# A hybrid S5 and stick-breaking attention block on Trainium2: the tiles on the left side of SBUF lie 32 bytes further on

## The chip, the cores and the metric

The kernel runs on one core of a Trainium2 chip (trn2). The metric is the device time of one execution in microseconds, and the kernel before takes 1482.84 us as the median of three runs (1481.27 to 1486.74). The engines are named as in the profile: PE is TensorE's matmuls and PEld its weight loads, DVE is VectorE, ACT is ScalarE, POOL is GpSimd, and SP issues most of the DMAs.

SBUF is the on-chip memory: 128 partitions, in each of which a tile has a start address in bytes. A matmul reads two operands from SBUF. The stationary one (128 columns here) is put into the array by a weight load; the streamed one then runs through it, up to 512 columns at a time. The result goes to PSUM.

## The reference

One layer, a sequence of 2048 tokens of width 1024, all in float32. From the reference, cut:

```python
hn = rmsnorm(h, mix_norm_g[i])
proj = hn @ w_in[i]
u, g_ssm, q, k, v, g_attn = jnp.split(proj, SPLITS, axis=-1)
y_ssm = s5_branch(u, ...) * jax.nn.silu(g_ssm)
y_att = stick_breaking_branch(q, k, v, q_norm_g[i], k_norm_g[i]) * jax.nn.silu(g_attn)
h = h + jnp.concatenate([y_ssm, y_att], axis=-1) @ w_out[i]
ple_gate = jax.nn.sigmoid(rmsnorm(h, ple_norm_g[i]) @ w_ple_gate[i])
h = h + ple_gate * (p[i] @ w_ple_proj[i])
```

The S5 branch is a diagonal complex state-space model in 32 groups, followed by a GELU and a gated linear unit. The attention has 8 heads of 64, and its weights are products of sigmoids over the keys between a key and the query.

## The kernel before, in words

**The products.** Matmuls that need more precision than one pass gives are done in three: both operands are split into a high and a low part (`split`, line 511; type float32r), and `mm3` and `mm3x` (lines 536 and 702) add high x high, high x low and low x high. So a group of matmuls stands on three lines of the profile: 541 to 543 for `mm3`, 707 to 709 for `mm3x`. Other matmuls are plain float32, and PE also does the transposes (lines 526, 340, 999).

**The stages, in order of time.**

- `phase_u` (line 546) loads x and the first weights and makes u (ps_u). The weights w_w are stationary, and the tokens xt, 256 columns at a time, are streamed.
- Eight batches of the state-space model (`ssm_pack`, `ssm_batch`), with `gate_unit` (line 642) between them: ps_sg, with w_w stationary and xt or xg streamed. Two blocks of attention projections (ps_qk, line 733) lie here too.
- Attention over four passes of two heads. `attn_proj` (line 712) makes q, k, v and the gate from tokens xt (stationary) and weights w_w (streamed, 512 columns): ps_q, line 745. It uses the array in two halves of 64 rows side by side, so its matmuls come in pairs. `attn_block` (line 795) makes the scores ps_z (line 812: q stationary, k streamed, in groups of three pairs), scans them on DVE (line 821), transposes them (ps_wt) and multiplies by v (ps_o, line 843).
- The gated linear unit, `glu_unit` (line 684), among the last attention blocks: ps_g and ps_v, with w_w stationary and zr streamed.
- `phase_out` (line 1037): `mixed_pair` makes ps_h from W_out and `gated_pair` ps_g from the gate's weights, both through `cross_products` (line 903), which needs seven half-size products instead of eight. Its stationary operand is yr, which is made from the tokens; the streamed one is a weight tile: w_w (products 0 to 3), wx (4) or w_wc (5 and 6). ps_p multiplies p by its weights: pr stationary, w_wp streamed.

**Where tiles lie.** Tiles come from pools. A pool opened without a side grows from the left end of SBUF upwards, one opened with `side="right"` from the right end downwards, and a pool that is closed leaves its room to the next. In order, the pools on the left are const, then w (the weights w_w, 16 tiles of 4096 bytes), stage, then gx with pu, stage1 or pb, later xp with kv2, wx and glu, at the end fin with fstage. On the right are kv0, proj, keep, chain or pack, later kv1 and attn, at the end w3, hr and gstage. The tiles that the matmuls read lie so:

| tile | pool | side | made or loaded at |
|---|---|---|---|
| w_w | w, wx | left | line 478 |
| xt, xg | gx, xp | left | 553, 589, 646, 716 |
| zr | glu | left | 674 |
| yr | fin | left | 916 |
| wx | xp | left | 888 |
| k | kv0 (slot 0), kv1 (1, 3, 4) | right | 769 |
| k | kv2 (slots 2, 5, 6, 7) | left | 769 |
| q | proj | right | 770 |
| w_wc, w_wp | w3 | right | 478 |
| pr | hr | right | 1005 |

The first pool, const, holds ten small tiles of a few bytes to 512 bytes a partition. Each takes a slot of whole multiples of 32 bytes. Everything on the left begins where const ends, so what const holds sets all the addresses on that side; pools on the right count from the other end (line 1331: `first, last = 16512, 229344`).

**The order of the work.** Each engine has its own queue. The order within each is not that of the code: the program's instructions are planned by a list scheduler (`plan`, `list_schedule`, `best_order`, `arrange`, lines 1328 to 1568), which takes costs from `duration` and dependencies from overlaps of tiles, and fixes the order on each engine.

The tile that the change touches is `warm` (lines 1081 to 1083). It is set to zero, and one sigmoid on it puts ACT's table in place at the start. Nothing reads it later.

Of the kernel before, what the change touches and what calls it, by code (L numbers as in the profile page):

```python
# [18 lines left out]
P = 128  # L19
# [1030 lines left out]
def hybrid_block_kernel(ctx: ExitStack, tc: tile.TileContext, x, xt, small, p, w_in, ssm_w_glu, w_out, w_ple_gate,  # L1050
# [27 lines left out]
    def const(name, shape, dt=F32):  # L1078
        return cp.tile(shape, dt, tag=name, name=name)

    warm = const("warm", [P, 1])
    nc.vector.memset(warm, 0.0)
    nc.scalar.activation(warm, warm, AF.Sigmoid)
    e.ident = const("ident", [P, P])
# [537 lines left out]
```

## Time and profile before

| what | value |
|---|---|
| time, median of three runs | 1482.84 us |
| the three runs | 1481.27, 1486.74, 1482.84 us |
| the profiled execution, span from its first to its last instruction | 1479.9 us |
| mean granted TensorE clock | 0.995 of full speed |
| DMA moved | 238.21 MB, 161 GB/s in the mean |

The profiled execution has no time of its own beside its span. The span leaves out what lies before the first and after the last instruction, and stands 2.9 us below the median.

In the groups of instructions, each row has the line, the engine, the operation, the tile written and the tiles read, the shapes, the number of instructions, and then after the bar the busy time of the group in us and the mean duration of one in ns, and behind the second bar the idle time of the engine just ahead of them with what ended it. In the timeline, each row has the start and the duration in us, then the engine, the line, the operation, the tiles, the shapes, and how many instructions were merged into the row. Matmuls are pipelined: the duration of one holds its way through the array, so the next one starts before it ends.

### The profile page before, as it was taken

How to read it: one execution, taken by the hardware profiler on the slowest of the kernel's cores; microseconds unless marked ns; L12 is line 12 of the kernel's file. 1: busy time of each engine (PE TensorE's matmuls, PEld its weight loads, DVE VectorE, ACT ScalarE, POOL GpSimd, SP SyncE). 2: the span in 40 equal slices, each digit the busy share in tenths (PEclk: the TensorE clock that was granted, in tenths of full speed). 3: DMA queues.
4: the chain of work that ended last, by engine and by line, in shares of the span. 5: the costliest groups of instructions: out<-in, count | busy, mean ns of one | idle time of the engine just before them, and what ended most of it. 6: DMA issues, size and time to landing. Idle time of an engine off the chain costs nothing.

```text
span 1479.9 us, 33585 instructions
## 1 busy us (share of the span) xinstructions
PE 1442.7 (97%) x13068; PEld 1222.7 (83%) x13068; DVE 1010.3 (68%) x1817; ACT 809.6 (55%) x1765; POOL 473.1 (32%) x512
## 2 busy tenths in 40 slices
PE   6999999999999999999999999999999999999998
PEld 5999889988888888888888877787777887777776
DVE  8953877977567886678766766665787557844444
ACT  5654555655555766566655755465655435533332
POOL 3121364422221212121122115443234554433432
PEclk9999999999999999999999999999999999999999
DMA  8886846644333433334333455766477546423221
GB/s 289 286 285 208 247 140 192 198 155 154 136 134 114 149 116 115 107 123 143 116 129 126 125 133 188 237 204 185 137 245 244 182 156 209 143 71 100 86 74 55
DMA packets 179054, 238.21 MB, mean 161 GB/s; under 512 B 65760, under 2 KB 121296, under 8 KB 167760
## 3 DMA queue, kind: packets, MB, share of 16 engines
q1 hardware_dynamic: 176512, 227.49, 47.5%
q0 software_dynamic: 2384, 8.59, 2.0%
q8 instruction: 103, 1.69, 0.5%
q14 instruction: 55, 0.45, 0.1%
HBM read 166.94 MB, written 64.90 MB: 157 GB/s over the span
## 4 chain that ended last, share of the span: by engine, by line
PE 79%; DVE 9%; issue 3%; ACT 3%; POOL 3%; DMA 2%; SPq 0%; POOLq 0%; DVEq 0%; ACTq 0%
PE ps_q L745 21%; PE ps_o L843 8%; PE ps_z L812 6%; PE ps_wt L526 4%; PE ps_g L707 4%; PE ps_h L707 3%; PE ps_h L709 3%; PE ps_h L708 3%; PE ps_g L709 3%; PE ps_g L708 3%; DMA v<-qn 2%; PE ps_u L541 1%; PE ps_u L543 1%; PE ps_u L542 1%; POOL sx L912 1%
## 5 line engine op out<-in xcount | busy, mean ns | idle before, releaser
L821 DVE TENSOR_TENSOR_SCAN px<-px,ps_z 128x512 f32<-128x512 f32 (+3 forms) x320 | 339.9, 1085 | 84.8 <-ACT px L816 61.5
L745 PE MATMUL ps_q<-w_w,xt 64*128 64x512 f32 x2784 | 375.6, 398 | 1.3 <-DVE qn L65 0.7
L745 PEld LDWEIGHTS ps_q<-w_w,xt 64*128 64x128 f32 x2784 | 269.7, 185 | 39.9 <-DVE qn L65 2.0
L816 ACT ACTIVATE px<-ps_z 128x512 f32<-128x512 f32 (+3 forms) x320 | 159.2, 536 | 80.8 <-PE ps_z L812 79.5
L835 ACT ACTIVATE ws<-ps_wt 128x512 f32<-128x512 f32 (+3 forms) x320 | 160.8, 539 | 72.0 <-PE ps_wt L526 67.1
L812 PE MATMUL ps_z<-k,q 64*128 64x512 f32 (+3 forms) x960 | 137.8, 379 | 3.6 <-DVE px L821 1.8
L843 PE MATMUL ps_o<-ws,v 128*64 128x128 f32 x2176 | 135.2, 276 | 0.0
L843 PEld LDWEIGHTS ps_o<-ws,v 128*64 128x64 f32 x2176 | 117.6, 137 | 17.8 <-issue 14.9
L507 POOL TENSOR_TENSOR rs_qk<-rs_qk,mhalf 128x4 f32<-128x4 f32 x64 | 67.6, 1057 | 155.0 <-DVE rs_qk L72 152.4
L526 PEld LDWEIGHTS ps_wt<-ident,px 64*128 64x128 f32 x2176 | 95.5, 138 | 24.6 <-issue 5.5
L812 PEld LDWEIGHTS ps_z<-k,q 64*128 64x128 f32 x960 | 87.9, 186 | 21.6 <-issue 5.6
L526 PE MATMUL ps_wt<-ident,px 64*128 64x64 f32 x2176 | 101.0, 224 | 1.9 <-ACT ws L835 1.8
L819 POOL TENSOR_SCALAR_AFFINE_SELECT px<-px 128x128 f32<-128x128 f32 x128 | 40.6, 327 | 166.5 <-ACT px L816 157.3
L756 POOL TENSOR_TENSOR v<-qn,v 128x128 f32<-128x128 f32 x64 | 32.2, 504 | 161.4 <-DMA v<-qn 146.9
L541 PE MATMUL ps_u<-xt,w_w 128*128 128x256 f32 x256 | 75.5, 296 | 8.2 <-ACT w_w L491 6.9
L65 DVE TENSOR_TENSOR yr<-sx,yr 128x512 fp32r<-128x512 f32 x64 | 50.7, 814 | 42.0 <-ACT yr L513 41.2
L543 PE MATMUL ps_u<-xt,w_w 128*128 128x256 f32 x256 | 74.1, 296 | 2.0 <-DVE w_w L76 2.0
L542 PE MATMUL ps_u<-xt,w_w 128*128 128x256 f32 x256 | 74.9, 294 | 0.5 <-DVE xt L65 0.5
L1031 POOL TENSOR_TENSOR sg<-sg,h 128x512 f32<-128x512 f32 x28 | 39.6, 1414 | 95.6 <-DVE sg L65 94.2
L513 ACT ACTIVATE yr<-sx 128x512 fp32r<-128x512 f32 x64 | 39.1, 627 | 55.5 <-POOL sx L912 25.8
L65 DVE TENSOR_TENSOR qn<-ps_q,part 128x512 f32<-128x512 f32 x54 | 36.8, 681 | 42.7 <-ACT part L751 39.1
L513 ACT ACTIVATE yr<-yq 128x512 fp32r<-128x512 f32 x48 | 30.3, 631 | 55.4 <-PE ps_h L709 23.3
(438 smaller groups left out, 3492.3 us busy)
## 6 DMA issues: line engine op xcount, KB each, us to landing
xt<-hn SPq DMA_DIRECT2D x58, 1024.0 KB
hn<-xt SPq DMA_DIRECT2D x16, 1024.0 KB
h<-h SPq DMA_DIRECT2D x64, 256.0 KB
wst<-in_w_in_dram SPq DMA_DIRECT2D x48, 256.0 KB
xg<-hn SPq DMA_DIRECT2D x12, 1024.0 KB
out_dram<-sg SPq DMA_DIRECT2D x31, 256.0 KB
x<-in_x_dram SPq DMA_DIRECT2D x14, 512.0 KB
h<-in_x_dram SPq DMA_DIRECT2D x28, 256.0 KB
```

Of the source, the lines that this page charges most:

```text
L526: e.nc.tensor.transpose(ps[h][:, 64 * k:64 * k + 64], v[r], e.ident[r, r])
L541: mm(out, wh, xh, start=first, stop=False)
L542: mm(out, wh, xl, start=False, stop=False)
L543: mm(out, wl, xh, start=False, stop=last)
L707: mm(out, xh, wh, start=first, stop=False, skip_group_check=more)
L708: mm(out, xh, wl, start=False, stop=False, skip_group_check=more)
L745: nc.tensor.matmul(o, xt[r, a, c], A.w[c][r, b], start=c + s == 0, stop=c == NC8 - 1 and s == 2)
L812: nc.tensor.matmul(z[:, :n], q[half[h], a], A.k[ch][half[h], b, :n], start=s == 0, stop=s == 2)
L816: nc.scalar.activation(px[:, :n], z[:, :n], AF.Sigmoid, scale=-(HD ** -0.5))
L821: nc.vector.tensor_tensor_scan(rv, rv, z[:, :n][:, ::-1], initial=1.0 if carry[h] is None else carry[h], op0=ALU.mult, op1=ALU.bypass)
L835: nc.scalar.activation(dst, ps, AF.Copy, bias=1.0, scale=-1.0)
L843: nc.tensor.matmul(po[half[h], :P], A.v[sb][:, h], w[:, h, b], start=sb == i, stop=sb == 0)
```

## The change

One line in `hybrid_block_kernel`. The tile `warm` is given 16 columns of float32 instead of one (64 bytes a partition instead of 4), and its first column is used as before. Its slot in const grows from 32 bytes to 64, and all that lies behind it on the left lies 32 bytes further on. The first weight tile moves from 17312 to 17344, which is a multiple of 64. Tiles on the right side stay where they are, and no instruction is added or taken away.

```diff
@@ -1078,7 +1078,7 @@
     def const(name, shape, dt=F32):
         return cp.tile(shape, dt, tag=name, name=name)
 
-    warm = const("warm", [P, 1])
+    warm = const("warm", [P, 16])[:, :1]
     nc.vector.memset(warm, 0.0)
     nc.scalar.activation(warm, warm, AF.Sigmoid)
     e.ident = const("ident", [P, P])
```

## The prediction

> **What bounds the kernel now.** I read the page first: engine totals, granted clock and the chain of waits.
>
> ```profile
> span 1479.9 us, 33585 instructions
> PE 1442.7 (97%) x13068; PEld 1222.7 (83%) x13068; DVE 1010.3 (68%) x1817; ACT 809.6 (55%) x1765; POOL 473.1 (32%) x512
> ...
> PEclk9999999999999999999999999999999999999999
> ...
> PE 79%; DVE 9%; issue 3%; ACT 3%; POOL 3%; DMA 2%; SPq 0%; POOLq 0%; DVEq 0%; ACTq 0%
> ```
>
> TensorE (PE) is busy 97% of the span at full granted clock, and 79% of the chain that ends last is matmuls. All the idle time of PE together is 1479.9 - 1442.7 = 37.2 us. So the kernel is as long as the stream of matmuls and their weight loads, and what matters is the spacing from one matmul to the next. Next I read the groups by line with shapes kept apart, for PE, to see which matmuls there are.
>
> ```profile
> L745 PE MATMUL ps_q<-w_w,xt 64*128 64x512 f32 x2784 | 375.6, 398 | 1.3 <-DVE qn L65 0.7 <-ACT part L751 0.5 <-DVE old L76 0.2
> L541 PE MATMUL ps_u<-xt,w_w 128*128 128x256 f32 x256 | 75.5, 296 | 8.2 <-ACT w_w L491 6.9 <-ACT xt L513 1.2
> L541 PE MATMUL ps_sg<-xg,w_w 128*128 128x256 f32 x192 | 55.6, 290 | 0.0
> L709 PE MATMUL ps_h<-w_w,yr 128*128 128x512 f32 x128 | 50.8, 397 | 0.0
> L707 PE MATMUL ps_qk<-w_w,xg 128*128 128x512 f32 x32 | 12.9, 404 | 0.0
> L745 PE MATMUL ps_q<-w_w,xg 64*128 64x512 f32 x96 | 12.4, 398 | 1.6 <-DVE gsq L65 1.6
> L541 PE MATMUL ps_g<-zr,w_w 128*128 128x512 f32 x64 | 26.2, 409 | 0.0
> L707 PE MATMUL ps_p<-w_wp,pr 128*128 128x512 f32 x64 | 25.4, 397 | 0.0
> L707 PE MATMUL ps_h<-w_wc,yr 128*128 128x512 f32 x64 | 25.4, 397 | 0.0
> L999 PE MATMUL ps_t<-ident,h 128*128 128x128 f32 x128 | 19.4, 273 | 0.2 <-ACT yq L1001 0.2
> L707 PE MATMUL ps_h<-wx,yr 128*128 128x512 f32 x32 | 12.7, 396 | 0.0
> L340 PE MATMUL ps_pack<-ident,bn 128*128 128x128 f32 x64 | 9.8, 272 | 0.2 <-DVE bn L65 0.2
> ```
>
> A mean of 397 ns is the latency of one matmul, its drain included, and not the spacing. The spacing is read from the starts in the timeline, in stretches where PE waits for nobody. The rows below are four such stretches (first and last row of each, the rows between left out), each a run of one kind of matmul.
>
> ```profile
> 970.26 0.39 PE L541 MATMUL ps_v<-zr,w_w 128*128 128x512 f32 x1
> ...
> 971.85 0.39 PE L542 MATMUL ps_v<-zr,w_w 128*128 128x512 f32 x1
> ```
> ```profile
> 1286.57 0.39 PE L707 MATMUL ps_p<-w_wp,pr 128*128 128x512 f32 x1
> ...
> 1287.26 0.39 PE L707 MATMUL ps_p<-w_wp,pr 128*128 128x512 f32 x1
> ...
> 1289.07 0.40 PE L709 MATMUL ps_p<-w_wp,pr 128*128 128x512 f32 x1
> ```
> ```profile
> 1130.81 0.40 PE L707 MATMUL ps_h<-w_wc,yr 128*128 128x512 f32 x1
> ...
> 1133.38 0.39 PE L709 MATMUL ps_h<-w_wc,yr 128*128 128x512 f32 x1
> ```
> ```profile
> 226.60 0.28 PE L541 MATMUL ps_sg<-xg,w_w 128*128 128x256 f32 x1
> ...
> 228.28 0.28 PE L543 MATMUL ps_sg<-xg,w_w 128*128 128x256 f32 x1
> ```
>
> Seven steps of ps_v take 1.59 us: 227 ns each. ps_p takes three steps of 230 ns and then eight in 1.81 us: 226 ns each; it settles. Eleven steps of ps_h from w_wc take 2.57 us: 234 ns, and that run never settles. Fourteen steps of ps_sg, half as wide, take 1.68 us: 120 ns. So the same 512-column matmul comes at two spacings, 227 and 234 ns, and the difference (6.7 ns, half of 13.4) is what an address could be responsible for. [...]
>
> ```profile
> 9.20 0.41 PE L541 MATMUL ps_u<-xt,w_w 128*128 128x256 f32 x1
> ...
> 12.62 0.41 PE L542 MATMUL ps_u<-xt,w_w 128*128 128x256 f32 x1
> ```
>
> Sixteen steps in 3.42 us are 213.8 ns for 256 columns at half clock: 106.9 ns at full clock. Against that, 120 and 227 ns carry 13 ns too much each (227 - 213.8 for 512 columns), and 234 ns carries 20.
>
> **Where the operands lie.** I worked the addresses out of the tile sizes (slots rounded up to 32 bytes, the first at 16512), and give them modulo 512, since nearly every tile is a multiple of 512 bytes and so keeps its pool's remainder. w_w, xt, xg and zr are at 416, wx too. yr is at 448, because a small tile (ss0) lies ahead of it in its pool. On the right side w_wc, w_wp, pr and q are at 480. What the timeline shows then has a simple rule: where the streamed operand and the stationary one have the same remainder (zr and w_w: 416 and 416; w_wp and pr: 480 and 480; xg and w_w) the stream settles at 227 or 120 ns; where they differ (w_wc and yr: 480 and 448) it stays at 234. It is the distance between the two that the spacing follows in these rows, not the remainder of either. The scores (ps_z) test this further, since their keys lie in three pools while q stays at 480.
>
> ```profile
> 601.62 2.31 PE L745 MATMUL ps_q<-w_w,xt 64*128 64x512 f32 x18
> 603.76 0.86 PE L812 MATMUL ps_z<-k,q 64*128 64x512 f32 x6
> 604.46 1.55 PE L745 MATMUL ps_q<-w_w,xt 64*128 64x512 f32 x12
> ...
> 774.94 2.35 PE L745 MATMUL ps_q<-w_w,xt 64*128 64x512 f32 x18
> 777.10 0.90 PE L812 MATMUL ps_z<-k,q 64*128 64x512 f32 x6
> 777.80 1.57 PE L745 MATMUL ps_q<-w_w,xt 64*128 64x512 f32 x12
> ```
>
> The first k is in pool kv1 at 384, a multiple of 64; the second in kv2 at 416, 32 bytes past one. Both take 0.70 us for their three pairs, 233 ns a pair, the spacing of operands that do not match. A streamed operand at a multiple of 64 bytes gained nothing there.
>
> **The change part by part.** It adds no instruction, no wait and no transfer; queues and their order stay. It adds 32 to every address on the left: 416 becomes 448, 448 becomes 480. The right side stays.
>
> 1. Pairs with both operands on the left: ps_q 2784 and 96 more from xg, so 1440 side-by-side pairs; ps_u and ps_sg 1536 (three lines of 256 each: 768 and 768); ps_g and ps_v from zr 384 (six lines of 64); ps_qk 96 (three of 32). Both remainders move from 416 to 448, the distance stays 0, so 227 and 120 ns stay: 0 us. The same for w_w and wx with yr (768 + 192): 416 and 448 become 448 and 480, still 32 apart: 0 us. Bounds for this part are the two steps seen: up to 6.7 ns a matmul either way, priced under the rivals.
> 2. w_wc with yr: 480 and 448 become 480 and 480. By the rule these 384 matmuls (192 in ps_h, 192 in ps_g) settle at 227. At most 384 x 6.7 ns = 2.6 us. They come in 16 groups of 24, and the ps_p run needs some steps to settle; with a quarter lost to that I take 1.9 us. It is all on PE's path, which ends last there.
> 3. ps_z with keys of kv2 (pool on the left): the distance goes from -64 to -32; both differ, and the kv1 row (distance -96) shows the same 0.70 us: 0, between -3 x 6.7 ns and +3 x 6.7 ns on each of the 56 groups that the slots of kv2 hold, 1.1 us either way.
> 4. Transposes: ident moves, their data does not. L999 (h at 480) and L340 (bn at 128) stand at 273 and 272 ns with different distances: 0.
> 5. The other engines and the DMA. DVE 68% and ACT 55% hide behind PE; a gain there could return at most the 37.2 us of PE's idle time, and a loss of a few ns an instruction stays hidden. The place without that cover is the start, where PE waits for the first weights.
>
> ```profile
> 0.00:60.00 60.00, 45.36 (x363) 41.80 (x364) 54.12 (x286) 36.93 (x63) 17.02 (x31) 0.91 0.81 281
> ...
> 600.00:900.00 300.00, 298.64 (x3660) 252.55 (x3658) 214.82 (x358) 184.17 (x443) 58.94 (x107) 1.00 0.41 125
> ```
>
> In the first 60 us (columns: PE, PEld, DVE, ACT, POOL busy, clock, DMA share, GB/s) PE idles 14.6 us and the DMA is 81% busy; later, in 600 to 900, PE idles 1.4 of 300 us. The rows loaded at the start are 1 to 2 KB long, and start at no multiple of 256 bytes before or after. I take 0, with 1 us either way.
>
> [...]
>
> Sum: 1482.8 - 1.9 = 1480.9, say **1481 us**. The profiled span is 1479.9, 0.2% below the median of 1482.8, so the trace's nanoseconds can be taken off the median as they are.
>
> [...]
>
> **The rivals.**
>
> *Aligned streams are cheaper.* That both operands are at a multiple of 64 bytes is seen nowhere in this trace, so a line of 64 bytes that is no longer split could give back one step of 6.7 ns in all of item 1: 3456 + 960 matmuls x 6.7 ns = 29.6 us, so 1482.8 - 29.6 = **1453 us**. The ends are 23 us (the matched 3456 alone, 1460) and the whole excess of 13 ns on 3456, 46 us (1437). For it: 13 ns a matmul are lost at full clock and none at half clock, so something in reading is short. Against it: the kv1 keys, aligned, at 233 ns a pair.
>
> [...]
>
> *A weight load from a multiple of 64 bytes is what costs 234 ns.* yr at 448 is the only stationary tile of these streams that starts at a multiple of 64, and both yr streams are the slow ones; the ps_z rows, where q at 480 is slow too, speak against it, but their runs are three pairs long. If it were so, from the first stationary tile that moves to 448 on, 3456 matmuls would go from 227 to 234 (+23.2 us) and the 1344 with yr from 234 to 227 (-9.0 us): +14.2 us, **1497 us**, and some 5 us less where ps_q has not settled anyway.
>
> *The change does nothing*, if slots were rounded to 64 bytes, so that warm takes the same room as before: 1482.8.
>
> **How the numbers follow.** About 0.5% (7.4 us) is what a measurement of this kernel can tell from no change. The rule of distance, with or without its 1.9 us, gets 0.50, no shift at all 0.03: both are within 0.5%, 0.53. Aligned streams get 0.28, all of it faster. Weight loads at multiples of 64 get 0.19, all slower. The likeliest is 1481, on its own from 1478 to 1485 (items 2, 3 and 5 at their ends). The range goes down to 1452, which takes in the rival's price of 29.6 us and its lower end but not the whole excess (about 0.1 left out), and up to 1497 for the slower rival (0.05 left out above).
>
> **What would show it.** Right: in the profile after, ps_v and ps_sg still step by 227 and 120 ns, ps_h from w_w still by 233 to 234, ps_h and ps_g from w_wc by 227 after a few steps, and the ps_z triples still take 0.70 us. Aligned streams: ps_v steps by 220 ns or less, ps_sg by less than 120, and the PE busy time falls by over 20 us. The slower rival: ps_v at 234 while ps_h from w_w falls to 227. Wrong in all of them: the matmul spacing stays, but the first 60 us or the DMA's share change by microseconds.

## The result, and the profile after

| | before | after |
|---|---|---|
| time, median of 21 runs each | 1483.51 us | 1480.82 us |
| lowest and highest | 1481.27 to 1486.74 | 1477.82 to 1483.06 |
| ratio, with its 95% interval | | 0.9981 [0.9974, 0.9987] |
| span of the profiled execution | 1479.9 us | 1481.3 us |
| granted clock, mean of that execution | 0.995 | 0.994 |

The change takes off 2.7 us (1483.51 - 1480.82; by the interval of the ratio between 1.9 and 3.9). That is real, and under the 0.5% that the prediction's chances counted as a change. The forecast was 1481 us, 1.9 us less than the 1482.8 that it started from.

The page of the profile after, in the same lines as before: span, engine totals, granted clock, share of the chain.

```profile
span 1481.3 us, 33585 instructions
PE 1443.0 (97%) x13068; PEld 1223.7 (83%) x13068; DVE 1007.7 (68%) x1817; ACT 810.5 (55%) x1765; POOL 473.8 (32%) x512
...
PEclk9999999999999999999999999999999999999999
...
PE 81%; DVE 7%; DMA 3%; ACT 3%; issue 3%; POOL 3%; SPq 1%; POOLq 0%; DVEq 0%; ACTq 0%
```

Nothing in it shows a gain: the two profiled spans even stand the other way round, by 1.4 us (the profiled execution of after is the slowest of its 21, 1483.06 us). The totals of one execution are too coarse for an effect of two or three microseconds, because the granted clock dips for a few microseconds, and not equally often in each execution. The windows of the profile show this (columns as in the prediction: PE, PEld, DVE, ACT and POOL busy, then the clock, the DMA's share and its GB/s). First before, then after, in the stage ahead of the ps_h matmuls.

```profile
940.00:980.00 40.00, 38.46 (x367) 31.22 (x367) 24.88 (x36) 20.06 (x44) 19.23 (x22) 1.00 0.65 223
980.00:1020.00 40.00, 38.87 (x387) 31.22 (x383) 23.98 (x33) 26.82 (x54) 16.79 (x16) 1.00 0.64 183
1020.00:1060.00 40.00, 38.20 (x301) 29.27 (x303) 29.73 (x39) 24.40 (x47) 13.33 (x15) 0.96 0.56 174
```
```profile
940.00:980.00 40.00, 37.57 (x325) 30.37 (x326) 21.54 (x32) 18.36 (x41) 17.48 (x21) 0.96 0.63 219
980.00:1020.00 40.00, 39.55 (x420) 32.74 (x417) 25.19 (x36) 27.88 (x56) 16.03 (x16) 1.00 0.69 193
1020.00:1060.00 40.00, 37.31 (x281) 28.47 (x280) 27.74 (x36) 23.80 (x45) 16.59 (x17) 0.96 0.52 161
```

The profiled run of before has one stretch at 0.96, that of after has two. Narrower windows show what such a stretch holds: a clock of 0.57 over 4 us. First before, then e3, an experiment below.

```profile
1023.00:1027.00 4.00, 4.00 (x21) 2.92 (x23) 3.31 (x4) 2.59 (x6) 1.50 (x2) 0.57 0.75 238
```
```profile
1024.00:1028.00 4.00, 4.00 (x44) 3.07 (x45) 3.37 (x4) 2.61 (x7) 1.94 (x2) 1.00 0.65 206
```

In both PE has just waited for DVE, 1.60 us at the longest, yet only before lost the clock. From 1020 to 1060 us the clock is 0.96 in before, after, e9 and e10 and 0.91 in e4, but 1.00 in e3. The second dip of after lies at 962 us (0.50 from 962 to 964). A dip of 0.04 over 40 us is worth up to 1.6 us, and the stretch from the first zr matmul to the first ps_h took 227.9 us before and 230.4 after. So the change has to be read from the spacing of matmuls and from a stage without such a dip. The last stage is one: from the first ps_h matmul (1093.1 us before, 1096.5 after, by the groups of ps_h) to the end of the span it takes 386.8 us before and 384.7 after. This is 2.1 us less, and there the change acts: added up from start to start, the ps_h and ps_g matmuls from w_wc give 2.0 of it, and every other group together 0.1.

The spacings after, from the timeline, in the order of the prediction: ps_v, ps_h from w_wc and then from w_w, ps_sg, and the scores.

```profile
973.64 0.39 PE L541 MATMUL ps_v<-zr,w_w 128*128 128x512 f32 x1
...
976.13 0.39 PE L543 MATMUL ps_v<-zr,w_w 128*128 128x512 f32 x1
```
```profile
1172.23 0.39 PE L707 MATMUL ps_h<-w_wc,yr 128*128 128x512 f32 x1
...
1173.61 0.39 PE L707 MATMUL ps_h<-w_wc,yr 128*128 128x512 f32 x1
...
1177.47 0.39 PE L709 MATMUL ps_h<-w_wc,yr 128*128 128x512 f32 x1
1177.69 0.40 PE L707 MATMUL ps_h<-w_w,yr 128*128 128x512 f32 x1
...
1180.96 0.40 PE L709 MATMUL ps_h<-w_w,yr 128*128 128x512 f32 x1
```
```profile
254.03 0.28 PE L541 MATMUL ps_sg<-xg,w_w 128*128 128x256 f32 x1
...
255.95 0.28 PE L542 MATMUL ps_sg<-xg,w_w 128*128 128x256 f32 x1
```
```profile
603.64 0.87 PE L812 MATMUL ps_z<-k,q 64*128 64x512 f32 x6
604.34 1.56 PE L745 MATMUL ps_q<-w_w,xt 64*128 64x512 f32 x12
...
778.03 0.86 PE L812 MATMUL ps_z<-k,q 64*128 64x512 f32 x6
778.73 1.55 PE L745 MATMUL ps_q<-w_w,xt 64*128 64x512 f32 x12
```

Eleven steps of ps_v take 2.49 us, 226 ns each: as before. The run of ps_h from w_wc begins with six steps of 230 ns in the mean (1.38 us), and then seventeen take 3.86 us, 227 ns each: it now settles, where it stood at 234 to its end before. The w_w run right behind it takes 3.27 us for fourteen steps, 234 ns: as before. Sixteen steps of ps_sg take 1.92 us, 120 ns: as before. Both score triples take 0.70 us. The groups of instructions show the same two streams in their mean durations, which also shrink a little when the operands match: the row for w_wc stood at 25.4 us and 397 ns before, and the one for w_w has not moved.

```profile
L709 PE MATMUL ps_h<-w_w,yr 128*128 128x512 f32 x128 | 50.8, 397 | 0.0
L707 PE MATMUL ps_h<-w_wc,yr 128*128 128x512 f32 x64 | 25.1, 392 | 0.0
```

### The profile page after: what moved, and what is told of

Its sections match the earlier page's. It is cut to its first block, busy times and chain, and to the rows that moved or that the text cites. A ratio compares the mean times of both kernels' runs of the same rounds, so it can differ in the third digit from the quotient of the medians.

```text
span 1481.3 us, 33585 instructions
## 1 busy us (share of the span) xinstructions
PE 1443.0 (97%) x13068; PEld 1223.7 (83%) x13068; DVE 1007.7 (68%) x1817; ACT 810.5 (55%) x1765; POOL 473.8 (32%) x512
## 4 chain that ended last, share of the span: by engine, by line
PE 81%; DVE 7%; DMA 3%; ACT 3%; issue 3%; POOL 3%; SPq 1%; POOLq 0%; DVEq 0%; ACTq 0%
PE ps_q L745 21%; PE ps_o L843 8%; PE ps_z L812 6%; PE ps_wt L526 4%; PE ps_g L707 4%; PE ps_h L707 3%; PE ps_h L709 3%; PE ps_h L708 3%; PE ps_g L709 3%; PE ps_g L708 3%; DMA v<-qn 2%; PE ps_u L541 1%; PE ps_u L543 1%; PE ps_u L542 1%; PE ps_sg L541 1%
## 5 line engine op out<-in xcount | busy, mean ns | idle before, releaser
L513 ACT ACTIVATE yr<-yq 128x512 fp32r<-128x512 f32 x48 | 30.3, 632 | 55.3 <-PE ps_h L709 25.4
```

## The experiments

The theory is the prediction's rule of distance (D): the spacing of a stream follows the distance in bytes from its stationary tile to its streamed one, and lies at 227 ns when that distance is 0. Three rivals stand against it: that a stationary tile at a multiple of 64 bytes costs 234 ns (S, a rule on the remainder of one address), that the gain came from another engine or the DMA and not from the spacing (O), and that it is enough for the two addresses to agree modulo a smaller number, 64 or 128 bytes. The experiments move a tile's address by giving an unused stretch to a small tile ahead of it. No instruction is added, and every engine keeps its order of work.

A difference of 1 to 7 us can be lost in one run's clock, so two figures are given for each: the ratio of the timed runs against the kernel before on the same chip, and the time from the first ps_h matmul to the end of the span ("last stage", 386.8 us before and 384.7 us after). The spacings are means over the steps in which PE waits for nothing, with two rows of a steady run quoted where a verdict rests on them. The last stage repeats well: from 1100 us on the clock is 1.00 in before, after, e1 and e3, and e3 and e10 below are the same kernel, with spans of 1471.6 and 1476.9 us, and both have a last stage of 379.6.

**e1: yr put at 416, where w_w, wx and the rest of the left lie.** On the kernel before. yr's distance to w_w and wx becomes 0, to w_wc 64.

```diff
-    ss = pool.tile([P, 2, 2], F32, tag=f"ss{j}", name="ss")
+    ss = pool.tile([P, 128 if j == 0 else 4], F32, tag=f"ss{j}", name="ss")[:, :4].rearrange("p (i m) -> p i m", i=2)
```

> The kernel before, with only yr moved: from 448 to 416, where w_w and wx lie (w_wc stays at 480). Theory D (the spacing follows the distance between streamed and stationary operand): ps_h and ps_g from w_w and wx step by 227 ns in place of 234, those from w_wc stay at 234: 960 x 6.7 ns = 6.4 us less than before, about 1477. Theory S (a weight load from a multiple of 64 bytes is what is slow): all 1344 matmuls with yr fall to 227, w_wc's too: 9.0 us less, about 1474.5. Theory O (the gain of the change came from elsewhere, the DMA or another engine, and the spacing is not what sets the end): no change within 1.5 us.

Measured: 1476.95 us against 1483.24, ratio 0.996 [0.9947, 0.9972]; last stage 381.1 us. The timeline of e1:

```profile
1159.61 0.39 PE L709 MATMUL ps_h<-w_w,yr 128*128 128x512 f32 x1
...
1162.11 0.39 PE L708 MATMUL ps_h<-w_w,yr 128*128 128x512 f32 x1
...
1171.88 0.39 PE L709 MATMUL ps_h<-w_wc,yr 128*128 128x512 f32 x1
...
1173.26 0.39 PE L709 MATMUL ps_h<-w_wc,yr 128*128 128x512 f32 x1
```

Eleven steps from w_w take 2.50 us, 227 ns; w_w and yr now match, and 5.7 us go from the last stage. The w_wc stream is a surprise: six steps in 1.38 us, 230 ns (steps of 226, 229 and 232 in turn), and it stays there. A distance of 64 has neither of the two spacings that the prediction knew. S had all 1344 matmuls with yr at 227 here, and O no change; the w_wc stream and the 5.7 us speak against them.

**e2: the change, and yr at 448, where the change puts w_w and wx.** On the kernel after, with the edit of e1. The stationary yr lies at a multiple of 64, as in before, and matches w_w; w_wc is 32 away.

> The kernel after, with yr moved back from 480 to 448, where w_w and wx now lie; w_wc is at 480. D: w_w and wx with yr step by 227 ns, w_wc with yr by 234 again; 6.4 us less than before, as in the run with yr at 416, about 1477. S: yr is at a multiple of 64 again, so all 1344 step by 234; as before, 1483.5. O: as after, about 1481.

Measured: 1479.97 us against 1483.24, ratio 0.9975 [0.9964, 0.9986]; last stage 382.4 us, 4.4 less than before. The timeline of e2:

```profile
1176.22 0.39 PE L707 MATMUL ps_h<-w_w,yr 128*128 128x512 f32 x1
...
1178.72 0.39 PE L709 MATMUL ps_h<-w_w,yr 128*128 128x512 f32 x1
...
1187.79 0.40 PE L707 MATMUL ps_h<-w_wc,yr 128*128 128x512 f32 x1
...
1190.35 0.40 PE L709 MATMUL ps_h<-w_wc,yr 128*128 128x512 f32 x1
```

With the same stationary yr, eleven steps from w_w take 2.50 us (227 ns) and eleven from w_wc 2.56 us (233 ns). S falls: a stationary tile at a multiple of 64 runs at 227 when its stream matches it. The time itself falls by 3.3 us (by the interval 2.1 to 5.3), where 6.4 was expected. The last stage shows the shortfall too: each of the 960 matmuls gives 4.6 ns (4.4 us / 960) and not 6.7. ps_g from w_w stands at 228.7 ns in the mean, not 227, because its runs need steps to settle. They do so behind an unmatched w_wc run, and behind the transposes as well, since e3 below, where w_wc matches, has 228.6 there. By the same working e1 has 4.5 ns for each (its 384 from w_wc, at 229.8 for 233.4, give 1.4 of its 5.7 us).

**e3: everything on 480.** On the kernel before: 64 bytes more on the left instead of 32, and the edit of e1 for yr, so that left and right, w_w, wx, w_wc and yr all match. Only the keys in kv1 (384) do not.

```diff
-    warm = const("warm", [P, 1])
+    warm = const("warm", [P, 24])[:, :1]
...
-    ss = pool.tile([P, 2, 2], F32, tag=f"ss{j}", name="ss")
+    ss = pool.tile([P, 128 if j == 0 else 4], F32, tag=f"ss{j}", name="ss")[:, :4].rearrange("p (i m) -> p i m", i=2)
```

> The kernel before, with the left side 64 bytes further on and yr put where w_w lies: w_w, xt, zr, wx, yr, w_wc, w_wp and pr all at 480, k of kv0 and kv2 too, and only k of kv1 at 384. D: every stream of ps_h and ps_g settles at 227; 1344 x 6.7 ns = 9.0 us less than before, less a little for settling, and some 1 us for the scores with keys of kv2: about 1474. S: 9.0 us less too (no stationary operand at a multiple of 64), so this run does not tell D from S; O: no change.

Measured: 1475.44 us against 1483.24, ratio 0.995 [0.9935, 0.9966]; last stage 379.6 us, 7.2 less than before. The timeline of e3:

```profile
1171.82 0.39 PE L707 MATMUL ps_h<-w_w,yr 128*128 128x512 f32 x1
...
1173.86 0.39 PE L707 MATMUL ps_h<-w_w,yr 128*128 128x512 f32 x1
```

Nine steps take 2.04 us, 227 ns, and ps_h and ps_g settle there from all three weights. Of the 1344 matmuls with yr (960 from w_w and wx, 384 from w_wc) each gives 5.4 ns (7.2 us / 1344) of the 6.7 between the two spacings; at least part of the rest is in the steps in which a stream settles (ps_g from w_w, 228.6 ns in the mean). The left side has gone from 416 to 480 and its matched streams are where they were (ps_q at 230.2 ns for 230.0), so neither remainder is better than the other.

**e4: the tokens and zr moved away from w_w.** On the kernel before: 32 bytes more for each of the two buffers that the weights land in, behind w_w, so that xt, xg, zr and wx lie at 480, w_w stays at 416, and yr lies at 0.

```diff
-            raw = e.stage[c % len(e.stage)].tile([P, 512], F32, tag="wst", name="wst")[:, :width]
+            raw = e.stage[c % len(e.stage)].tile([P, 520], F32, tag="wst", name="wst")[:, :width]
```

> The kernel before, with the tokens xt, xg and zr moved by 64 bytes against the weights (480 against 416), yr at 0. All distances of ps_u, ps_sg, ps_qk, ps_g and ps_v from zr, and five sixths of ps_q become 64 or -64; every operand is where it was modulo 64. D with all of the distance: ps_v, ps_g from zr and ps_qk settle at 233 to 234 in place of 227, ps_q's mean of 230 rises to 233; 480 x 5 ns + 1200 x 3.3 ns = 6.4 us more, and between 0 and 1536 x 6.7 ns = 10.3 us more for ps_u and ps_sg, whose mismatched spacing no run has shown: 6 to 17 us more, 1490 to 1500. D modulo 64 (only the remainders modulo 64 have to agree): no change, 1483.5. S and O: no change.

Measured: 1487.32 us against 1483.24, ratio 1.0024 [1.0012, 1.0035], slower by 1.8 to 5.2 us. The timeline of e4: ps_u, ps_qk, ps_sg, ps_v.

```profile
114.83 0.28 PE L541 MATMUL ps_u<-xt,w_w 128*128 128x256 f32 x1
...
116.99 0.28 PE L542 MATMUL ps_u<-xt,w_w 128*128 128x256 f32 x1
...
219.44 0.40 PE L707 MATMUL ps_qk<-w_w,xg 128*128 128x512 f32 x1
...
222.24 0.40 PE L707 MATMUL ps_qk<-w_w,xg 128*128 128x512 f32 x1
...
252.27 0.28 PE L542 MATMUL ps_sg<-xg,w_w 128*128 128x256 f32 x1
...
254.98 0.28 PE L541 MATMUL ps_sg<-xg,w_w 128*128 128x256 f32 x1
...
973.44 0.39 PE L541 MATMUL ps_v<-zr,w_w 128*128 128x512 f32 x1
...
975.96 0.39 PE L543 MATMUL ps_v<-zr,w_w 128*128 128x512 f32 x1
```

All four streams were matched before and are 64 apart now, with different signs. Where the streamed operand lies 64 below the stationary one (ps_qk, w_w on xg), twelve steps take 2.80 us, 233 ns. Where it lies 64 above (ps_v, zr streamed on w_w), eleven take 2.52 us, 229 ns. In ps_qk as in ps_v the two operands differ by 64, so they agree modulo 64: the rival that this is enough falls, since it would leave both at 227. The half-wide streams do what no theory expected: nineteen steps of ps_u take 2.16 us, 113 to 114 ns, and twenty-three of ps_sg take 2.71 us, 118 ns, less than the 120 of matched operands. This gives part of the loss back, which is why the loss is smaller than the 6 to 17 us expected: up to the first ps_q from xt the run is 1.6 us ahead of before (336.0 us for 337.6). The loss itself is mostly ps_q: its 1440 pairs go from 230.0 to 232.9 ns in the mean, 4.2 us. The trace agrees: from that first ps_q to the first zr matmul it takes 531.5 us, and 527.6 to 528.9 in the five runs (before, e1, e6, e7, e8) whose operands lie as in before until then.

**e5: the kv1 keys on 480 too.** On e3, with 112 columns instead of n for the small tile `r` in `rms_rstd` when its tag is "qk". What it tells apart: whether a mismatched score triple costs only its own 7 ns a pair, or also makes the following ps_q stream settle anew.

> The run with everything at 480, and the keys of kv1 moved from 384 to 480 as well (the tile rs_qk ahead of q is padded, q stays at 480): every streamed and every stationary operand of the float32r matmuls is at 480. D (the spacing follows the distance): the ps_z pairs with keys of kv1 fall from 233 to 230 ns as those of kv0 and kv2 have, and ps_q, which no longer meets a mismatched group, needs less settling and falls from 230 towards 227: between 1 and 5 us less than with the keys of kv1 at 384, so 1470 to 1474. A rival, that settling after a stall costs the same whatever ran before: ps_q stays at 230, 1 us less at most, 1474 to 1475.

Measured: 1477.34 us against 1482.03, ratio 0.997 [0.9961, 0.9979]; e3 had 0.995 on another chip, so no further gain is to be seen. The score pairs from kv1 go from 232.9 to 230.4 ns, and ps_q only from 230.2 to 229.8, 0.6 us over its 1440 pairs. So ps_q settles anew behind a score triple whether that triple matched or not.

**e6, e7, e8: yr at 288, 160 and 384.** On the kernel before, the edit of e1 with 96, 64 and 120 columns instead of 128. They map the spacing against the distance: to w_w and wx it becomes 128, 256 and 32, to w_wc 192, 320 and 96.

> The kernel before with yr at 288: w_w and wx lie 128 ahead of yr, w_wc 192 ahead. The runs before showed 227 ns at a distance of 0, 229 at +64, 234 at +32, -32 and -64. If distance 0 is the best there is (D in its narrow form), both streams step by 229 to 234, and the time is between 1477 and 1484. If only the remainder modulo 128 counts, w_w and wx step by 227 and w_wc by 229 to 234: about 1477. If the spacing falls the further the streamed operand is ahead, both are under 227, down to the 213.8 that the stream itself takes: up to 960 x 20 + 384 x 20 ns = 27 us less, 1457 at the least.

> The kernel before with yr at 160: w_w and wx lie 256 ahead of yr, w_wc 320 ahead (or 192 behind). Narrow D: both step by 229 to 234, 1477 to 1484. Modulo 128 or 256: w_w and wx step by 227, about 1477. Further ahead is better: both under 227, down to 1457.

> The kernel before with yr at 384, a multiple of 128: w_w and wx lie 32 ahead of yr, w_wc 96 ahead. Narrow D and the rule by remainders both: w_w and wx step by 233 to 234 (as w_wc did before, 32 ahead), w_wc by 229 to 234: as before or 2 us less, 1481 to 1484. Further ahead is better: w_wc under 229, and w_w still at 234.

Measured, against 1482.03 us: e6 1482.4, ratio 1.0004 [0.9995, 1.0013], last stage 386.3; e7 1475.97, ratio 0.9964 [0.9952, 0.9976], last stage 381.0; e8 1483.47, ratio 1.0016 [1.0004, 1.0029], last stage 387.0. The timelines of e7, then e6, then e8:

```profile
1169.19 0.39 PE L707 MATMUL ps_h<-w_wc,yr 128*128 128x512 f32 x1
...
1170.57 0.39 PE L707 MATMUL ps_h<-w_wc,yr 128*128 128x512 f32 x1
...
1184.24 0.39 PE L707 MATMUL ps_h<-wx,yr 128*128 128x512 f32 x1
...
1186.74 0.39 PE L709 MATMUL ps_h<-wx,yr 128*128 128x512 f32 x1
```
```profile
1185.60 0.40 PE L707 MATMUL ps_h<-wx,yr 128*128 128x512 f32 x1
...
1188.16 0.39 PE L709 MATMUL ps_h<-wx,yr 128*128 128x512 f32 x1
```
```profile
1188.68 0.39 PE L707 MATMUL ps_h<-w_wc,yr 128*128 128x512 f32 x1
...
1194.04 0.39 PE L709 MATMUL ps_h<-w_wc,yr 128*128 128x512 f32 x1
```

In e7 eleven steps at a distance of 256 take 2.50 us, 227 ns, and six steps at 320 take 1.38 us, 230 ns: the spacings of distances 0 and 64, and the last stage is that of e1 (381.0 and 381.1). So the rule repeats after 256 bytes, at the two distances tried. At 128 (e6) eleven steps take 2.56 us, 233 ns; at 96 (e8) twenty-three take 5.36 us, 233 ns. So it is not enough to agree modulo 128, and a stream further ahead is not faster, two rivals that e6's expectation had named. Put together, for 512 columns, by the distance of the streamed operand ahead of the stationary one modulo 256:

| distance | 0 | 32 | 64 | 96 | 128 | 160 | 192 | 224 |
|---|---|---|---|---|---|---|---|---|
| ns | 227 | 233 | 229 to 230 | 233 | 232 to 233 | 234 | 233 | 233 |
| seen in | e1, e2, e3, e7 | before, e2, e8 | e1, e4, e7 | e8 | e6 | e4 | e4, e6 | before, after |

Each is the mean of the steady part of its streams: the one at 160 is yr against w_w in e4 (416), the one at 224 yr against w_w in before and after (-32).

**e9 and e10: the half-wide streams at 64.** e9 is e3 with 64 bytes more in gx, ahead of xt and xg, so that ps_u, ps_sg and ps_qk run at a distance of 64 from the weights and all later stages are matched. e10 is e3 once more, on the same chip.

```diff
-    e.row = [gx.tile([P, 256], F32, tag=f"row{T}", name=f"row{T}") for T in range(1)]
+    e.row = [gx.tile([P, 272], F32, tag=f"row{T}", name=f"row{T}")[:, :256] for T in range(1)]
```

> The run with everything at 480, and the tokens of pool gx (ps_u, ps_sg; also ps_qk and 96 matmuls of ps_q) put 64 bytes ahead of the weights, as in the run with the tokens moved by 64. D with its table of distances: ps_sg steps by 118 ns in place of 120 and ps_u by 113 to 118; 768 x 2 ns = 1.5 us less up to the first ps_q from xt, up to 5 us less if ps_u settles at 113 where the DMA lets it; ps_qk and ps_q from xg step by 233 (0.5 us more). ps_h and ps_g stay at 227. In all 1 to 3 us less than the run with everything at 480. Rival: the stage before the first ps_q from xt waits for the first loads and for the chains between the state-space batches, so its end does not move: same as everything at 480.

> The run with everything at 480 once more, on one chip with the run above, so that the two can be told apart. D: 7 to 9 us less than before, from the first ps_h to the end some 7 us less.

Measured, against 1482.67 us: e9 1475.88, ratio 0.9956 [0.9943, 0.997]; e10 1477.35, ratio 0.9965 [0.9951, 0.9978]. The timeline of e9:

```profile
71.30 0.28 PE L541 MATMUL ps_u<-xt,w_w 128*128 128x256 f32 x1
...
73.91 0.28 PE L543 MATMUL ps_u<-xt,w_w 128*128 128x256 f32 x1
...
164.68 0.28 PE L542 MATMUL ps_sg<-xg,w_w 128*128 128x256 f32 x1
...
168.92 0.28 PE L542 MATMUL ps_sg<-xg,w_w 128*128 128x256 f32 x1
```

Twenty-three steps of ps_u take 2.61 us, 113 ns, and thirty-six of ps_sg take 4.24 us, 118 ns: the short spacings of e4 are there again, without its losses in the later stages. The first ps_q from xt starts at 336.1 us, 1.4 us earlier than in e10 (337.5). But e3, the same kernel as e10, starts it at 336.6, so 0.9 of the 1.4 us is within what one execution differs from the next. The medians differ by 1.5 us, as expected, but their intervals overlap, so the spacing is shown and the gain in time is not. The lowest ratios are 0.995 and 0.9965 for the kernel of e3 and e10, and 0.9956 for e9, against 0.9981 for the change alone; the intervals of e1 and e7 (0.996 and 0.9964), which move only yr, overlap with theirs.

## Why the prediction was right

The mechanism that it named is what the runs show: the matmuls from w_wc step faster, and the other long streams do not. That the time came within 0.2 us of the forecast is luck: over 21 runs before stands at 1483.5 us and not at the 1482.8 of its first three, and the gain is 2.7 us and not 1.9, and the two differences cancel.

*Item 1, both operands moved together: 0 us.* Shown by the profile after: ps_v 226 to 227 ns, ps_sg 120, ps_h from w_w 234. The mean spacing of ps_q is 230.0 ns before and 230.1 after. The change brings the weights to multiples of 64 bytes, but no stream in which both operands move sees it; e3 puts the same streams on 480, a multiple of 32 only, and they stay as well.

*Item 2, w_wc and yr: 1.9 us of at most 2.6.* The mechanism is shown, by the rows of ps_h from w_wc after and by e2, which takes the match away again and has 233 ns there. The size is 2.1 us by the last stage of the trace and 2.7 us by the medians. The mean spacing falls from 233.4 to 228.1 in ps_h and 227.4 in ps_g, so 192 matmuls each give about 5 and 6 ns, 2.2 us. The allowance of a quarter for settling was a little too much: the run quoted above spends six of its 23 steps at 230 in the mean instead of 234, and the others at 227. In ps_g the 24 come as twelve and twelve, with ps_p between them, and the second twelve stand at 227 from their start.

*Item 3, the scores.* The triples quoted take 0.70 us as before, and the pairs from kv2 go from 233.3 to 233.0 ns. One thing was not foreseen: pairs from the kv0 keys, which match q before and after, went from 232.7 to 229.8. What runs ahead of them (ps_q, w_w and xt) has moved by 32; why this should matter was not tried. At 2.9 ns for each, the 84 pairs from kv0 give 0.2 us at most.

The kv0 pairs also take something from the prediction's argument. It read the unmatched triples at 0.70 us as a test of the rule, and as a word against aligned streams. But kv0 lies at 480, as q does, and its triples in before take the same:

```profile
349.33 0.96 PE L812 MATMUL ps_z<-k,q 64*128 64x512 f32 x6
350.03 0.49 PE L745 MATMUL ps_q<-w_w,xt 64*128 64x512 f32 x2
```

So in before matched and unmatched triples could not be told apart, and three pairs were too short a run to decide anything. The forecast for the scores held, but what the prediction could rest its rule on were the long runs of ps_v, ps_sg, ps_p and ps_h alone.

*Items 4 and 5, transposes, other engines, transfers.* No difference to be told from one run to the next: PE is busy 1443.0 us for 1442.7, DVE 1007.7 for 1010.3, and the first 60 us have the DMA at 80% for 81%, with 45.34 us of PE for 45.36.

```profile
0.00:60.00 60.00, 45.34 (x362) 41.64 (x363) 54.01 (x285) 36.98 (x63) 17.05 (x31) 0.91 0.80 282
```

*The rivals.* Aligned streams are no cheaper: ps_v has both operands at 448 after the change and stays at 227, so no run shows the line of 64 bytes that this rival supposed. A weight load from a multiple of 64 costs nothing: ps_v loads w_w from 448 in the kernel after, and e2 has yr at 448 with 227. That the change does nothing is excluded by the w_wc run (227 ns for 234). The rival of aligned streams took its upper end from an excess of 13 ns a matmul, reckoned from 213.8 ns for 256 columns at half clock. The rows behind that figure lie at 9 to 13 us, where the profile of before has the granted clock at 1.00, so they do not show half clock by themselves. The same step stands at a granted clock of 0.50: 22 steps from 35.25 us take 4.69 us, 213 ns each. The lowest steady spacings that the runs showed are 226 to 227 ns for 512 columns (ps_v after, e3) and 113 for 256 (e4, e9).

*Where the rule was too coarse.* The prediction had two spacings, matched and not. There is a third: a streamed operand 64 bytes (or 320) ahead of the stationary one steps at 229 to 230, and with 256 columns even below the matched 120 (113 and 118 in e4 and e9). The prediction could not have read this from before, where no stream has that distance. It cost nothing here, because the change makes no such pair, but it is why e4 came out below the 6 us that its expectation began with. The direction matters too: 64 behind is 233 (ps_qk in e4).

With the same instructions and the same stationary tile the spacing is 227 or 233 ns by where the streamed tile lies (e2). The author's guess from it, which no run tests, is that the reads of the weights and of the stream get in each other's way. In the timeline the two reads that run together belong to two matmuls: after, the stream of one starts at 1173.61 us and the weight load of the next at 1173.62. In a steady run both stationary tiles lie alike, so the runs do not tell whether a stream's own weights count or the next ones. Nor is it shown where that would be, and why 64 ahead should help was not settled.

## What to carry to other kernels

When TensorE is the bound and its matmuls each come with a weight load, read the spacing from the starts in the timeline and set it against where both operands lie; here moving one tile so that stationary and streamed operands agree modulo 256 bytes was worth up to 3% of each matmul concerned (227 for 234 ns), and 0.4% of the kernel (e1, e7). Moving both operands together changed nothing here (ps_v at 227 ns before and after), and neither did it matter that an address is a multiple of 64 bytes (227 ns at 448 in e2, at 480 in e3). An effect of a few microseconds has to be read from spacings and from a stage whose granted clock is the same in both runs, not from the two spans.

## What the hardware showed that was not expected

- The spacing of 512-column matmuls follows the distance of their operands, is the same at 256 bytes as at 0 (227 ns) and at 320 as at 64 (230 ns, e7), and stands at 232 to 234 ns at 32, 96, 128, 160, 192 and 224.
- At a distance of 64 the 256-column matmuls are faster than matched ones (120 ns), and have two steady spacings, 113 and 118 ns, in the same kernel (e9: ps_u and ps_sg).
- A matched stream does not always start at 227 ns: behind the unmatched wx, ps_h from w_wc takes six steps at 230 in the mean (after), and ps_p takes three (before). ps_q, cut into short runs by the scores, stays at 230.0 to 230.3 in every run that matches it except e5 (229.8).
- The granted clock drops for a few microseconds (0.57 over 4 us above, and 0.50 from 1024 to 1026 us in it), which costs an estimated 1.7 us (0.43 of 4 us). The dip at 1023 us comes behind a wait of PE of 1.60 us, but the same wait in e3 brought none. By that estimate two such dips more or fewer move a span by 3.4 us, more than this change does (2.7).
